# Seven half-block products for the middle half of an output projection, with the weight sums made in DRAM

## The chip, the cores and the metric

The kernel runs on one core of a Trainium2 chip. Its engines are TensorE (PE, with its weight loads shown as PEld), VectorE (DVE), ScalarE (ACT), GpSimd (POOL) and the queue engine SyncE (SP), which issues nearly all DMAs. The metric is the device time of one execution in microseconds (us), as the median of several.

## The reference

The reference is one decoder layer on 512 tokens of width 2048. It normalizes the input, projects it with `w_in`, runs two groups of eight attention heads of width 128 side by side (latent attention with a rotary key, and forgetting attention with a decay in the logits), multiplies each head's output with a SiLU gate, and projects the 16 heads together back to 2048 columns:

```python
o = jnp.concatenate([o_mla, o_fox], axis=-1) @ w_out      # (512 x 2048) @ (2048 x 2048)
return x + _rms_norm(o, g_post)
```

All of it is float32. The change touches the product with `w_out` only.

## The kernel before

**Stages.** The four pairs of forgetting heads come first (loop over `p` at L718: projections of values, queries, keys and gates, with the attention of the pair before woven in between), then the latent projections (L779), the gates of the latent heads (L841), the four pairs of latent heads (L867), and last the output projection (L988). The text counts the pairs from 0; pair 0 of the forgetting heads is first.

**Products in three terms.** A float32 operand is split in a rounded part `hi` and a remainder `lo`, and `mm3` (L128) issues hi x hi, hi x lo and lo x hi, three matmuls of 512 columns on one bank of PSUM. `split_into` (L118) makes the parts: ACT casts the rounded one, DVE subtracts it for the remainder.

**Weights.** All weights come in chunks of at most 1024 columns per partition, 512 KB. `chunk(i)` (L231) loads four chunks ahead on SP's queue into tiles `raw` (3 buffers) and divides two chunks ahead into `whi` and `wlo` (3 buffers each): an ACT cast (L220) and a DVE subtraction (L221). A division can't write before PE is done with the chunk that had the buffer, and a load can't land before the division of the chunk that had its buffer.

**The projection.** Each of the four blocks of 512 output columns runs over 16 contraction tiles (one head each; the forgetting heads first) and 4 token tiles. A chunk of `w_out` holds two contraction tiles, so a block has 8 chunks and 16 x 4 x 3 = 192 matmuls. The attention of the last latent pair is woven into block 0 by `pump` (L350), which takes steps from the list `todo`. After each block and token tile, `square` (L942) sums the squares on ACT and `gain` (L946) multiplies with the gain row on DVE. After block 3, `finish` (L953) scales the four pieces of a token tile, adds the residual rows `xr` and stores them.

**Memory.** 28 slots of 4 KB per partition (`slot`, L95) hold the head outputs, their split parts, the gain rows and the gained pieces. Once block 0 is done, the pools of the attention are closed and a pool `op` takes their place (L1024); tile by tile it waits for what stood there. Before, it held the residual rows only.

**Order.** Each engine works through its own list in order. Outside one stretch written out by hand (L718 on, first pair), the framework that builds the program makes these lists: it plays the program through with estimated durations, gives an idle engine the ready instruction that stands first in the program, and places the waits. So an instruction may run well ahead of its place in the text where its inputs and its tile are free.

Of the kernel before, what the change touches and what calls it, by code (L numbers as in the profile page):

```python
# [24 lines left out]
HW = 128  # L25
NH = 8
# [37 lines left out]
def tile_hybrid_layer(  # L64
# [16 lines left out]
    nc = tc.nc  # L81
    pe, act, dve, pool = nc.tensor, nc.scalar, nc.vector, nc.gpsimd
# [5 lines left out]
    inner = ctx.enter_context(ExitStack())  # L88
# [39 lines left out]
    def mm3(o, ah, al, bh, bl, first, last, **kw):  # L128
        pe.matmul(o, ah, bh, start=first, stop=False, **kw)  # L129
        pe.matmul(o, ah, bl, start=False, stop=False, **kw)  # L130
        pe.matmul(o, al, bh, start=False, stop=last, **kw)  # L131
# [54 lines left out]
    def add_chunks(w, cols, nk, per, width, first_k=0, single=0):  # L186


        first = len(chunks)
        k = 0  # L190
        while k < nk:
            n = min(1 if k < single else per, nk - k)
            chunks.append((w, cols, (first_k + k) % nk, n, width))
            k += n
        return range(first, len(chunks))

# [2 lines left out]
    def load(i, small=None):  # L199

        w, cols, k, n, width = chunks[i]
        if i < 2:
            raw = slot(f"raw{i}", shape=(P, 1024))
        else:
            raw = wp.tile([P, 1024], F32, tag="raw", name=f"raw{i}")
        v = raw[:, : n * width].rearrange("p (k c) -> p k c", k=n)
        for at, off, cnt in cols:
            (nc.sync if cnt >= P or small is None else small).dma_start(
                v[:, :, at : at + cnt],
                w[0, k * P : (k + n) * P, off : off + cnt].rearrange("(k p) c -> p k c", p=P),  # L210
            )
        raws[i] = raw
# [18 lines left out]
    def chunk(i, ahead_load=4, ahead=2):  # L231
        while state["loaded"] < min(len(chunks), i + ahead_load + 1):
            load(state["loaded"])
            state["loaded"] += 1
        prepare(i + ahead)
        return ready.pop(i)
# [34 lines left out]
            }  # L271
        )

    outc = [add_chunks(w_out, [(0, 512 * p, 512)], NK, 2, 512, NH) for p in range(4)]


    gcol = cst.tile([P, NK + 10], F32, name="gcol")
# [72 lines left out]
    def pump(n=1):  # L350
        for _ in range(n):
            if todo:
                todo.popleft()()

    def drain():
        while todo:
            todo.popleft()()

    def proj_T(rng, outs, kh, kl, rate=1):

        k = 0
        n_k = sum(chunks[i][3] for i in rng)
        for i in rng:
            hi, lo = chunk(i)
            for j in range(chunks[i][3]):
                for o, rows, pick in outs:
                    mm3(o[:rows, :], pick(hi, j), pick(lo, j), kh[k], kl[k], k == 0, k == n_k - 1)
                k += 1
                pump(rate)

    def proj_V(rng, banks, kh, kl, rate=1):

        k = 0
        n_k = sum(chunks[i][3] for i in rng)
        for i in rng:
            hi, lo = chunk(i)
            for j in range(chunks[i][3]):
                for t in range(NT):
                    o, fst = piece_of(banks, t, chunks[i][4])
                    ts = slice(t * P, (t + 1) * P)  # L380
                    mm3(
                        o, kh[k][:, ts], kl[k][:, ts], hi[:, j, :], lo[:, j, :],
                        k == 0 and fst, k == n_k - 1, skip_group_check=True,
                    )
                k += 1
                pump(rate)

    def piece_of(banks, t, width):

# [530 lines left out]


    order = [o_of[n // 2][:, n % 2, :] for n in range(2 * NH)]
    gps = [slot(f"gp{c}") for c in range(2)]
    gp = [gps[c // 2][:, c % 2, :] for c in range(4)]
    for c in range(4):
        nc.sync.dma_start(gp[c], g_post[:, c * 512 : (c + 1) * 512].to_broadcast([P, 512]))
    parts = {}

    def o_parts(n):
        if n not in parts:  # L930
            parts[n] = split(order[n], f"os{n}")
        return parts[n]

    og = [[None] * 4 for _ in range(NT)]
# [5 lines left out]
    og_of, xr_of = {}, {}  # L940

    def square(t, c, o):  # L942
        jt = wp.tile([P, S], F32, tag="sq", name=f"osq{c}{t}", bufs=1)
        act.activation(jt, o, AF.Square, accum_out=sso[:, t, c : c + 1])

    def gain(t, c, o):  # L946

        if t % 2 == 0:
            og_of[t // 2, c] = slot(f"og{c}{t}")
        og[t][c] = o if c == 3 or t == NT - 1 and c > 0 else og_of[t // 2, c][:, t % 2, :]  # L950
        dve.tensor_tensor(out=og[t][c], in0=o, in1=gp[c], op=ALU.mult)

    def finish(t, o):  # L953
        v, y, w, u, h = (cst.tile([P, 1], F32, name=f"fin{s}{t}") for s in "vywuh")
        dve.tensor_reduce(out=u, in_=sso[:, t, 0:3], op=ALU.add, axis=AX.X)
        dve.tensor_scalar(out=u, in0=u, scalar1=1.0 / D, scalar2=EPS, op0=ALU.mult, op1=ALU.add)
        square(t, 3, o)
        dve.tensor_scalar(out=v, in0=sso[:, t, 3:4], scalar1=1.0 / D, scalar2=u, op0=ALU.mult, op1=ALU.add)
        act.sqrt(w, v)
        dve.tensor_scalar(out=h, in0=v, scalar1=-0.5, scalar2=None, op0=ALU.mult)  # L960
        gain(t, 3, o)
# [18 lines left out]
    def load_xr(t):  # L980
        for c in range(4):
            if c % 2 == 0:
                xr_of[t] = op.tile([P, 2, S], F32, tag="xr", name=f"xr{t}{c}", bufs=8)
            xr[t][c] = xr_of[t][:, c % 2, :]
            nc.sync.dma_start(xr[t][c], x[piece(t, c)])

    last = 3
    for c in range(4):  # L988
        ob = [att_bank(f"o{c}{t}") if t == NT - 1 and c in (1, 2) else proj_bank(f"o{c}{t}") for t in range(NT)]
        rng = list(outc[c])  # L990
        held = rng[-last:] if c == 3 else []
        n = 0

        def products(t, hi, lo, n, j):
            oh, ol = o_parts(n)
            ts = slice(t * P, (t + 1) * P)
            mm3(ob[t], oh[:, ts], ol[:, ts], hi[:, j, :], lo[:, j, :], n == 0, n == 2 * NH - 1)

        if c == 3:
            load_xr(0)  # L1000
        for i in rng[: len(rng) - len(held)]:
            hi, lo = chunk(i)
            for j in range(2):
                if n == 2 * NH - 2 and c == 0:
                    drain()
                for t in range(NT):
                    products(t, hi, lo, n, j)
                n += 1
                pump(2)
        if held:  # L1010
            w = [chunk(i, ahead=0) for i in held]
            for t in range(1, NT):
                load_xr(t)
        for t in range(NT):
            for m in range(2 * len(held)):
                products(t, *w[m // 2], n + m, m % 2)
            if held:
                finish(t, ob[t])
            else:
                square(t, c, ob[t])  # L1020
                gain(t, c, ob[t])
        if c == 0:
            inner.close()
            op = ctx.enter_context(tc.tile_pool(name="op", bufs=1, reuse_waits="tile"))  # L1024


# [33 lines left out]
```

## Time and profile before

| | us |
|---|---|
| median of 3 executions | 943.79 (943.67 to 945.33) |
| the profiled execution | 945.21 |
| its span | 943.1 |
| PE busy | 932.8 |
| DVE busy | 500.8 |
| ACT busy | 343.4 |
| POOL busy | 22.6 |
| output projection, first to last matmul | 748.0 to 934.3 |

The span runs from the first to the last instruction of the profiled execution. Matmuls are pipelined, so that one is shown with 389 ns although they follow each other faster; the pace is read from the distance of events that wait for PE. "Idle before, releaser" in a row is the time in which the engine stood still before these instructions and what ended it.

### The profile page before, as it was taken

How to read it: one execution, taken by the hardware profiler on the slowest of the kernel's cores; microseconds unless marked ns; L12 is line 12 of the kernel's file. 1: busy time of each engine (PE TensorE's matmuls, PEld its weight loads, DVE VectorE, ACT ScalarE, POOL GpSimd, SP SyncE). 2: the span in 40 equal slices, each digit the busy share in tenths (PEclk: the TensorE clock that was granted, in tenths of full speed). 3: DMA queues.
4: the chain of work that ended last, by engine and by line, in shares of the span. 5: the costliest groups of instructions: out<-in, count | busy, mean ns of one | idle time of the engine just before them, and what ended most of it. 6: DMA issues, size and time to landing. Idle time of an engine off the chain costs nothing.

```text
span 943.1 us, 11667 instructions
## 1 busy us (share of the span) xinstructions
PE 932.8 (99%) x4568; PEld 792.0 (84%) x4568; DVE 500.8 (53%) x898; ACT 343.4 (36%) x639; POOL 22.6 (2%) x28
## 2 busy tenths in 40 slices
PE   9999999999999999999999999999999999999996
PEld 8888888998889888888888888888888888888885
DVE  3477743467742743742322348668887973332325
ACT  5772432233312522321211253535445642232224
POOL 1000000000000000000000040000000000000003
PEclk9999999999999999999999999999999999999999
DMA  9343323332233332333333333322222324622214
GB/s 296 87 114 110 94 86 90 112 90 83 74 105 108 90 90 80 100 90 111 90 92 110 89 90 84 93 60 73 62 73 73 112 68 148 203 96 90 94 63 179
DMA packets 88474, 95.48 MB, mean 101 GB/s; under 512 B 12482, under 2 KB 72412, under 8 KB 88420
## 3 DMA queue, kind: packets, MB, share of 16 engines
q1 hardware_dynamic: 87684, 94.35, 33.4%
q8 instruction: 36, 0.59, 0.3%
q10 hardware_dynamic: 736, 0.40, 0.2%
q14 instruction: 18, 0.15, 0.1%
HBM read 90.52 MB, written 4.21 MB: 100 GB/s over the span
## 4 chain that ended last, share of the span: by engine, by line
PE 97%; DVE 2%; ACT 0%; issue 0%; DVEq 0%; ACTq 0%
PE o L129 6%; PE o L131 6%; PE o L130 6%; PE fv L418 4%; PE l L130 4%; PE l L129 4%; PE l L131 4%; PE fg L129 3%; PE fq L129 3%; PE fq L131 3%; PE fq L130 3%; PE fg L130 3%; PE gm L129 3%; PE fg L131 3%; PE fk L131 3%; PE fk L129 3%
## 5 line engine op out<-in xcount | busy, mean ns | idle before, releaser
L221 DVE TENSOR_TENSOR wlo<-raw,whi 128x1024 fp32r<-128x1024 f32 (+3 forms) x157 | 186.4, 1189 | 299.8 <-ACT whi L220 295.2
L220 ACT CAST whi<-raw 128x1024 fp32r<-128x1024 f32 (+3 forms) x157 | 158.9, 1013 | 410.5 <-PE o L131 94.9
L129 PE MATMUL o<-whi,os 128*128 128x512 f32 x256 | 100.6, 393 | 0.0
L130 PE MATMUL o<-wlo,os 128*128 128x512 f32 x256 | 99.8, 390 | 0.0
L131 PE MATMUL o<-whi,os 128*128 128x512 f32 x256 | 99.3, 390 | 0.0
L129 PE MATMUL l<-h,whi 128*128 128x512 f32 x160 | 62.2, 389 | 0.0
L130 PE MATMUL l<-h,whi 128*128 128x512 f32 x160 | 62.2, 389 | 0.0
L131 PE MATMUL l<-h,wlo 128*128 128x512 f32 x160 | 62.2, 389 | 0.0
L131 PEld LDWEIGHTS o<-whi,os 128*128 128x128 f32 x256 | 48.0, 188 | 10.3 <-DVE os L121 0.2
L130 PEld LDWEIGHTS o<-wlo,os 128*128 128x128 f32 x256 | 48.1, 188 | 9.8
L129 PEld LDWEIGHTS o<-whi,os 128*128 128x128 f32 x256 | 48.1, 188 | 9.7
L129 PE MATMUL fq<-h,whi 128*128 128x512 f32 x128 | 52.7, 412 | 0.0
L129 PE MATMUL fg<-h,whi 128*128 128x512 f32 x128 | 50.4, 394 | 0.0
L131 PE MATMUL fq<-h,wlo 128*128 128x512 f32 x128 | 50.2, 392 | 0.0
L130 PE MATMUL fq<-h,whi 128*128 128x512 f32 x128 | 50.2, 392 | 0.0
L129 PE MATMUL fk<-h,whi 128*128 128x512 f32 x128 | 50.1, 391 | 0.0
L130 PE MATMUL fg<-h,whi 128*128 128x512 f32 x128 | 50.0, 390 | 0.0
L131 PE MATMUL fg<-h,wlo 128*128 128x512 f32 x128 | 49.9, 390 | 0.0
L129 PE MATMUL gm<-h,whi 128*128 128x512 f32 x128 | 49.9, 390 | 0.0
L131 PE MATMUL gm<-h,wlo 128*128 128x512 f32 x128 | 49.9, 389 | 0.0
L131 PE MATMUL fk<-h,wlo 128*128 128x512 f32 x128 | 49.8, 389 | 0.0
L130 PE MATMUL gm<-h,whi 128*128 128x512 f32 x128 | 49.8, 389 | 0.0
(319 smaller groups left out, 1841.3 us busy)
## 6 DMA issues: line engine op xcount, KB each, us to landing
raw<-in_w_in_dram SPq DMA_DIRECT2D x88, 512.0 KB, 3.6
raw<-in_w_out_dram SPq DMA_DIRECT2D x32, 512.0 KB, 3.6
raw<-in_w_ukv_dram SPq DMA_DIRECT2D x8, 512.0 KB, 4.0
xr<-in_x_dram SPq DMA_DIRECT2D x16, 256.0 KB, 5.2
out_dram<-og SPq DMA_DIRECT2D x15, 256.0 KB, 2.6
xa<-in_x_dram SPq DMA_DIRECT2D x7, 512.0 KB, 7.2
raw<-in_w_in_dram SPq DMA_DIRECT2D x8, 384.0 KB, 3.2
raw<-in_w_uq_dram SPq DMA_DIRECT2D x24, 128.0 KB, 2.2
```

What stands on the lines that cost most here:

```text
L129: pe.matmul(o, ah, bh, start=first, stop=False, **kw)
L130: pe.matmul(o, ah, bl, start=False, stop=False, **kw)
L131: pe.matmul(o, al, bh, start=False, stop=last, **kw)
L220: act.copy(hi[:, :m], raw[:, :m])
L221: dve.tensor_tensor(out=lo[:, :m], in0=raw[:, :m], in1=hi[:, :m].bitcast(F32), op=ALU.subtract)
L418: pe.matmul(banks[t][:, :n], a[k][:, tss[t]], b[:, j, :], start=k == 0 and m == 0, stop=k == NK - 1 and m == 2,)
```

## The change

The columns 512 to 1535 of the product, so far two blocks of 512, are computed together as a 2 x 2 block product by the scheme of Winograd and Strassen. Tokens 0 to 255 and 256 to 511 are the row halves of the heads' output A, head pairs `K1` = 0, 1, 4, 5 and `K2` = 2, 3, 6, 7 its column halves, and `w_out` has the same halves of rows and the two blocks as columns. Seven products of 256 tokens, 1024 contraction rows and 512 columns take the place of eight. In the order in which they run: p1 = A11 B11, p4 = A22 t4, p2 = A12 B21, q6 = s6 t6, g5 = s5 t5, g7 = s7 t7, g3 = s3 B22, where

- t7 = B12 + B22, t5 = B11 + B12, t6 = B11 + t7, t4 = B21 + t6 (weights),
- s5 = A21 - A22, s6 = A11 - s5, s3 = A12 - s6, s7 = A21 - A11 (heads),
- C11 = p1 + p2, C21 = p4 + p1 - (q6 + g7), C12 = q6 - p1 + (g5 + g3), C22 = g5 - p1 + (q6 + g7).

A product that stands second in a bracket goes on adding in the same PSUM bank; the rest is combined by DVE. Blocks 0 and 3 stay as they are.

The weight sums are made in DRAM, four pieces of 512 KB for each, 16 in all. `add_blocks` issues for one piece a 64-byte DMA from a weight tile in SBUF into the destination (a marker, which ties the step to its place in the program), a copy of the first operand on SP, both DRAM to DRAM apart from the marker, and a DMA from POOL that adds the second operand. `behind` issues one such step at every eighth contraction tile of the projections, once the first pair of heads is done: `proj_T` and `proj_V` call it. The head sums are made by `sum_steps`: per pair of head pairs 4 subtractions and 4 splits, the two groups of forgetting heads during block 0 (written to slots), the two of latent heads during p1 and p4 (raw sums in PSUM banks, parts in the pool `op`). The pool `op` now has 13 tiles and also holds the gain rows, loaded after block 0 in the program, the gained pieces of block 0 and four groups of parts. The number of `w_out` chunks goes from 32 to 44.

```diff
+    K1, K2 = (0, 1, 4, 5), (2, 3, 6, 7)
+    def add_blocks(name, j, first, second, mark):
+        to = W[name][j].rearrange("p (k c) -> p k c", k=2)
+        nc.sync.dma_start(W[name][j][0:1, 0:16], mark)
+        nc.sync.dma_start(to, first)
+        pool.dma_start(to, second, accum_op=ALU.add)
...
+        for step in (
+            ("t7", j, b12, b22), ("t5", j, b11, b12), ("t6", j, b11, chain["t7"]), ("t4", j, b21, chain["t6"]),
+        ):
+            bg.append(lambda mark, step=step: add_blocks(*step, mark))
...
+    outc = {0: add_plain(range(NH), 0)}
+    outp = {
+        "p1": add_plain(K1, 1), "p4": add_sums("t4"), "p2": add_plain(K2, 1), "q6": add_sums("t6"),
+        "g5": add_sums("t5"), "g7": add_sums("t7"), "g3": add_plain(K2, 2),
+    }
+    outc[3] = add_plain(range(NH), 3)
...
+    def behind(k, w):
+        if done and bg and k % 8 == 0:
+            bg.popleft()(w[0:1, 0, 0:16].bitcast(F32))
...
-    gps = [slot(f"gp{c}") for c in range(2)]
...
+        def make(n, x, y):
+            raw[n] = raw_of(f"{n}{j}").rearrange("p (h c) -> p h c", h=2)
+            dve.tensor_tensor(out=raw[n], in0=x, in1=raw[y] if isinstance(y, str) else y, op=ALU.subtract)
+        def part(n):
+            both = place(f"s{n}{j}").rearrange("p x (h c) -> p x h c", h=2)
+            split_into(both[:, 0], both[:, 1], raw[n])
+            sums[n][j] = both
+        return [
+            lambda: make("g5", a21, a22), lambda: make("q6", a11, "g5"), lambda: part("g5"), lambda: part("q6"),
+            lambda: make("g3", a12, "q6"), lambda: part("g3"), lambda: make("g7", a21, a11), lambda: part("g7"),
+        ]
...
              pump(2)
+            if n >= 4:
+                for _ in range(2):
+                    if steps:
+                        steps.popleft()()
...
+    inner.close()
+    op = ctx.enter_context(tc.tile_pool(name="op", bufs=13, reuse_waits="tile"))
+    gps = [late(f"gp{c}") for c in range(2)]
...
+    def product(name, of, o, first, last):
+        kk = 0
+        for i in outp[name]:
+            hi, lo = chunk(i)
+            for j in range(2):
+                for t, (ah, al) in enumerate(of(kk)):
+                    mm3(o[t], ah, al, hi[:, j, :], lo[:, j, :], first and kk == 0, last and kk == 7,
+                        skip_group_check=True)
+                kk += 1
+                pump()
...
+    for j in range(2, 4):
+        todo.extend(sum_steps(j, bank_temp, lambda n: late(n, F32R)))
+    product("p1", block((0, 1), K1), A, True, True)
+    p1 = slot("p1")
+    for t in range(2):
+        act.copy(p1[:, t, :], A[t])
+    B = [proj_bank(f"ob{t}") for t in range(2)]
+    product("p4", block((2, 3), K2), B, True, True)
+    f = og_of[1, 1] = slot("c21")
+    for t in range(2):
+        dve.tensor_tensor(out=f[:, t, :], in0=B[t], in1=p1[:, t, :], op=ALU.add)
+    product("p2", block((0, 1), K2), A, False, True)
...
+    product("g7", summed("g7"), C, False, True)
+    homes = {c: att_bank(f"oh{c}") for c in (1, 2)}
+    for t in range(2):
+        dve.tensor_tensor(out=e[:, t, :], in0=C[t], in1=e[:, t, :], op=ALU.add)
+        dve.tensor_tensor(out=f[:, t, :], in0=f[:, t, :], in1=C[t], op=ALU.subtract)
+    for t in range(2):
+        for c, o in ((1, f), (2, e)):
+            square(2 + t, c, o[:, t, :])
+            gain(2 + t, c, o[:, t, :], homes[c] if t else None)
+    product("g3", summed("g3"), G, False, True)
```

More of the change, by code (lines that the diff above doesn't have):

```diff
@@ L938, in piece, with late @@
         return (0, slice(t * P, (t + 1) * P), slice(c * 512, (c + 1) * 512))
-    og_of, xr_of = {}, {}
+    def late(name, dt=F32, shape=(P, 2, S)):
+        return op.tile(list(shape), dt, tag="e", name=name)
+    og_of, xr_of, gp = {}, {}, {}
     def square(t, c, o):
@@ new lines, in tile_hybrid_layer, with block, of @@
+    while steps:
+        steps.popleft()()
+    inner.close()
+    op = ctx.enter_context(tc.tile_pool(name="op", bufs=13, reuse_waits="tile"))
+    gps = [late(f"gp{c}") for c in range(2)]
+    for c in range(4):
+        gp[c] = gps[c // 2][:, c % 2, :]
+        nc.sync.dma_start(gp[c], g_post[:, c * 512 : (c + 1) * 512].to_broadcast([P, 512]))
+    for t in range(NT):
+        square(t, 0, ob[t])
+        gain(t, 0, ob[t], place=late)
+    def block(tokens, half):
+        def of(kk):
+            n = 2 * half[kk // 2] + kk % 2
+            return [tuple(a[:, t * P : (t + 1) * P] for a in o_parts(n)) for t in tokens]
+        return of
@@ L1008, in tile_hybrid_layer @@
[L1008 to L1024, printed above, removed]
+                for t, (ah, al) in enumerate(of(kk)):
+                    mm3(
+                        o[t], ah, al, hi[:, j, :], lo[:, j, :], first and kk == 0, last and kk == 7,
+                        skip_group_check=True,
+                    )
@@ L1028 @@
+    n = 0
+    load_xr(0)
+    for i in rng[:-last]:
+        hi, lo = chunk(i)
+        for j in range(2):
+            for t in range(NT):
+                products(ob[t], t, hi, lo, n, j)
+            n += 1
+    w = [chunk(i, ahead=0) for i in held]
+    for t in range(1, NT):
+        load_xr(t)
+    for t in range(NT):
+        for m in range(2 * last):
+            products(ob[t], t, *w[m // 2], n + m, m % 2)
+        finish(t, ob[t])
 _INS = [
```

125 lines of the change are left out of this document (98 added, 27 removed).

## The prediction

> **What bounds the kernel now.** I read four views in this order: the page, the waits of PE, the busy time of each engine by stage, and the timelines of ACT and DVE in the output projection. The page comes first (engine: busy time and share), then its chain:
>
> ```profile
> span 943.1 us, 11667 instructions
> PE 932.8 (99%) x4568; PEld 792.0 (84%) x4568; DVE 500.8 (53%) x898; ACT 343.4 (36%) x639; POOL 22.6 (2%) x28
> PE 97%; DVE 2%; ACT 0%; issue 0%; DVEq 0%; ACTq 0%
> ```
>
> PE is busy for 99% of the span and is 97% of the chain. The waits of PE (who waited for whom, total, times, longest) are two, both in the first microseconds, and PEld has one of 0.2 us:
>
> ```profile
> PE warm L148 <- DVE warm L143: 1.1, 1, 1.1
> PE xt L306 <- DVE h L124: 0.7, 1, 0.7
> PEld o L131 <- DVE os L121: 0.2, 1, 0.2
> ```
>
> So every matmul taken away shortens the run, as long as the other engines still feed PE. Busy time by stage (length; then PE, PEld, DVE, ACT, POOL; granted clock, DMA share, GB/s) shows what room they have:
>
> ```profile
> 125.00:334.00 209.00, 209.00 (x1100) 183.08 (x1099) 111.70 (x211) 67.16 (x117) 0.00 (x0) 1.00 0.33 94
> 759.00:770.00 11.00, 11.00 (x59) 9.46 (x58) 10.39 (x28) 5.07 (x13) 0.00 (x0) 1.00 0.31 98
> 770.00:803.00 33.00, 33.00 (x158) 27.51 (x157) 10.96 (x15) 9.31 (x16) 0.00 (x0) 1.00 0.41 133
> 803.00:889.00 86.00, 86.00 (x381) 71.22 (x380) 24.96 (x24) 21.30 (x30) 0.00 (x0) 1.00 0.36 121
> 889.00:934.00 45.00, 45.00 (x200) 37.29 (x199) 18.84 (x42) 16.54 (x30) 5.37 (x5) 1.00 0.26 90
> ```
>
> The first row is forgetting pairs 1 and 2, where the new DMAs go; the next two are the first column block of the projection with the last attention heads; the fourth is the two middle blocks that change. There DVE works 25 us of 86, ACT 21, and the DMA engines are at 36%.
>
> **The gain.** The ACT timeline of the middle blocks (start, duration, line, what; in brackets the idle time before) shows the pace:
>
> ```profile
> 809.58 1.05 ACT L220 CAST whi<-raw 128x1024 fp32r<-128x1024 f32 x1 [3.68 <-PE o L131]
> 815.02 1.05 ACT L220 CAST whi<-raw 128x1024 fp32r<-128x1024 f32 x1 [4.38 <-PE o L131]
> 820.46 1.05 ACT L220 CAST whi<-raw 128x1024 fp32r<-128x1024 f32 x1 [4.38 <-PE o L131]
> ```
>
> Each cast waits until PE has finished a chunk, and they come every 5.44 us. A chunk is 2 contraction tiles x 4 token tiles x 3 terms = 24 matmuls, so a matmul costs 5.44 / 24 = 0.2267 us. Before, the middle takes 8 half-block products of 8 x 2 x 3 = 48 matmuls, 384 in all (87.0 us). After it takes 7 x 48 = 336. **Removed: 48 x 0.2267 = 10.9 us of PE.** The new matmuls have the same 512-column shape, so I give them the same price.
>
> **What feeding costs now.** A chunk serves only two token tiles in the half products, so PE eats one every 2.72 us, and there are 28 chunks in place of 16. Durations of the other engines by group, and then one division and one square from the timelines:
>
> ```profile
> L221 DVE TENSOR_TENSOR wlo<-raw,whi 128x1024 fp32r<-128x1024 f32 x16 | 19.6, 1225 | 58.1 <-ACT whi L220 58.1
> L220 ACT CAST whi<-raw 128x1024 fp32r<-128x1024 f32 x17 | 17.9, 1053 | 60.0 <-PE o L131 60.0
> L951 DVE TENSOR_TENSOR og<-o,gp 128x512 f32<-128x512 f32 x10 | 6.9, 692 | 5.6 <-ACT osq L944 5.4
> L121 DVE TENSOR_TENSOR os<-gm,os 128x512 fp32r<-128x512 f32 x8 | 5.5, 683 | 0.0
> L120 ACT CAST os<-gm 128x512 fp32r<-128x512 f32 x8 | 4.7, 644 | 0.2 <-DVE gm L505 0.2
> 810.66 1.23 DVE L221 TENSOR_TENSOR wlo<-raw,whi 128x1024 fp32r<-128x1024 f32 x1 [3.51 <-ACT whi L220]
> ...
> 802.10 0.60 ACT L944 ACTIVATE osq<-o 128x512 f32<-128x512 f32 x1 [2.30 <-PE o L131]
> 802.59 0.19 ACT L944 ACTIVATION_READ_ACCUMULATOR osq<-o 128x1 f32 x1
> ```
>
> A division takes 1.08 + 1.23 = 2.31 us from cast to remainder. It starts when PE frees one of three buffers and must end two chunks later, 5.44 us: a margin of 3.1 us. Stage totals fit: DVE 28 x 1.225 + 12 combining additions and 12 gains x 0.692 + 16 sum steps of heads 4 to 7 x 0.683 = 62 us of 76; ACT 28 x 1.053, 12 squares at 0.79, 8 casts x 0.644 and 2 copies = 45 us. What can hurt is bunching.
>
> *First two products.* DVE: 8 divisions 9.8, the 16 sum steps 10.9, 4 gains 2.8, 2 additions 1.4 = 24.9 us in 21.8. The excess, 3.1 us, equals the margin, and the planner can put part of the sums earlier, since DVE idles 22 us of 770 to 803. I take 0.5 us; bounds 0 and 3.1. The copy of the first product needs a free slot, which the sums of the third pair group give back; it waits in ACT's queue with the next casts behind it, inside the same bounds.
>
> *After the sixth product*, 4 additions and 4 gains (5.5 us of DVE) start 0.7 us before that product's end and stand before a division: 5.5 - 0.7 + 1.2 = 6.0 us against 5.44. I take 0.9 us; bounds 0 and 2.
>
> *First column block.* Sixteen more sum steps of the forgetting heads: 10.9 us on DVE, 8 x 0.64 = 5.2 on ACT, into the 22 and 24 us that are idle from 770 to 803. Cost 0. Placed in 759 to 770, where DVE is busy 10.39 of 11 us, the eight steps of one group would delay what they precede by 5.4 us; with the margin of 3.1 that is at most 2.3 us.
>
> The gain rows move to memory that the closed attention pools give back:
>
> ```profile
> 793.23 0.69 DVE L505 TENSOR_TENSOR gm<-pvm,gm 128x512 f32<-128x512 f32 x1 [5.04 <-PE pvm L499]
> 802.82 2.87 DVE L951 TENSOR_TENSOR og<-o,gp 128x512 f32<-128x512 f32 x4 [1.76 <-ACT osq L944]
> gp<-in_g_post_dram SPq DMA_DIRECT2D x4, 256.0 KB, 5.1
> ```
>
> The attention ends at 793.2 us, they land 5.1 us after issue, and the first gain runs at 802.8, which leaves 4.5 us. A late one would hold DVE's queue, with the divisions behind it.
>
> *Loads.* Three raw buffers; a cycle is issue 0.37 + landing + division 2.31. Landing times, first in the middle blocks, then as groups (16 residual rows; 5 weight loads from 785 to 812 us, with the rate of that stretch; 7 inputs at the start):
>
> ```profile
> DMA to landing us min/median/max: 3.6/3.7/5.0
> xr<-in_x_dram SPq DMA_DIRECT2D x16, 256.0 KB, 5.2
> raw<-in_w_out_dram SPq DMA_DIRECT2D x5, 512.0 KB, 4.5
> DMA packets 3358, 6.24 MB, mean 231 GB/s; under 512 B 314, under 2 KB 314, under 8 KB 3358
> xa<-in_x_dram SPq DMA_DIRECT2D x7, 512.0 KB, 7.2
> L208 SPq DMA_DIRECT2D raw<-in_w_out_dram x13: 368/368/379, 787.9 to 855.4; - x13
> ```
>
> At 3.7 us the pace is (0.37 + 3.7 + 2.31) / 3 = 2.13 us, at 5.0 it is 2.56, both under 2.72. The rate needed is 512 KB / 2.72 us = 193 GB/s. The residual rows, 4 MB, now wait for tiles that products 4 to 7 free: groups of 1 MB between loads, each delaying one load about 3.2 us (at 324 GB/s: 133 / 0.41 in the stage table), which the margin absorbs. Cost 0; upper bound below, with 7.2 us.
>
> *Forgetting heads.* The queries' first weight loads of pair 1 and of pair 3 (count, durations, first and last start), the smallest weight loads by landing time, and POOL's first work after the start:
>
> ```profile
> L129 PEld LDWEIGHTS fq<-h,whi x17: 187/188/190, 125.6 to 139.9; 128*128 128x128 f32 x17
> L129 PEld LDWEIGHTS fq<-h,whi x14: 187/188/190, 333.5 to 344.7; 128*128 128x128 f32 x14
> raw<-in_w_uq_dram SPq DMA_DIRECT2D x24, 64.0 KB, 2.1
> L800 POOL TENSOR_TENSOR ls<-ls,lqq 128x512 f32<-128x512 f32 x5 | 6.6, 1318 | 540.9 <-ACT lqq L798 540.6
> ```
>
> Sixteen steps, at every eighth contraction tile of pairs 1 and 2, so one in 209 / 16 = 13 us. Each puts on SP a 64-byte marker from a weight tile and a 512 KB copy that waits for the marker (about 2.1 us, the landing time of the smallest weight loads), and on POOL an adding DMA that waits for the copy. Behind them on SP stand the weight loads; a raw buffer has 3 x 5.44 - 2.31 = 14.0 us to be filled, less 0.37 + 3.7, so 9.9 us to spare. Behind them on POOL stands nothing until 540.9 us. The sums are first read near 810 us. No row shows an adding DMA. Lower bound: 3.6 us like a plain 512 KB load; I know no upper one, only the point at which it matters (rival 3). I take 0, nearest to the plain load. [...]
>
> **Sum.** -10.9 + 0.5 + 0.9 = -9.5 us. The profiled execution took 945.21 us (943.1 span and 2.1 around it), 1.4 above the median of 943.79. On the median: **934.3 us**.
>
> **Rivals.**
> 1. *Bunching bites deeper.* Upper bounds together: 3.1 + 2 + 2.3 = 7.4, plus a late residual group or so; 937 to 942 us. For it: DVE at 95% or more through two products, and order fixed ahead. Against: margins of 3.1 us per chunk, and DVE idle for 22 us just before.
> 2. *Loads set the pace of the middle* (slower). Place: the three raw buffers. If a 512 KB load lands in 7.2 us, as at the kernel's start, the pace is (0.37 + 7.2 + 2.31) / 3 = 3.29 us and 28 chunks lose 28 x 0.57 = 16 us: 943.8 - 10.9 + 16 = **949 us**. It decides from a landing time of 6.65 us, where the loss is 0.39 a chunk. For it: 193 GB/s plus 4.2 MB of residual rows over four products (43.5 us, 96 GB/s) is 289. Against: 4.5 us at 231 GB/s in 785 to 812.
> 3. *Adding DMAs starve the forgetting heads.* If copy and addition hold the engines so long that loads wait over 9.9 us in each of 16 steps, PE stops there. An addition of 12 us, beside 1.6 for the copy, would cost 16 x (12 + 1.6 - 9.9) = 59 us at most, less what interleaves; 945 to 990. Against: 33% DMA share, and 13 us between steps.
> 4. *The change doesn't do what it says:* PE's matmuls fall by 48 but the middle ends when it did, a new wait taking 9 to 12.8 us: 942 to 945.7.
>
> **How the numbers follow.** Forecast, 932.5 to 937: 0.60. Rival 1, 937 to 942: 0.21. Rival 4: 0.06. Rival 2: 0.08. Rival 3: 0.05. Low end: the whole 10.9 us and nothing lost is 932.9, less the spread of runs, 932.0. The high end takes in rival 1, 942.0; that leaves out 0.19. Within 0.2% is 941.9 to 945.7, which is what a measurement of this kernel can't tell from no change: 0.06. Faster 0.60 + 0.21 = 0.81; slower 0.08 + 0.05 = 0.13.
>
> **What would show it.** Right: 48 matmuls fewer; PE still busy at 99%; casts in the middle 2.72 us apart; no PE wait for whi or wlo over 2 us; raw loads landing under 5 us; the forgetting pairs still ending near 334 us. Wrong: PE waiting on wlo in every chunk with DVE idle (loads, rival 2) or DVE busy (rival 1); the stage 125 to 334 longer (rival 3); clock below 1.00 where PE pauses.

## The result and the profile after

| | before | after |
|---|---|---|
| median, us | 944.44 (943.67 to 945.33, 4 executions) | 932.08 (931.93 to 932.79, 4 executions) |
| the profiled execution, us | 945.21 | 932.0 |
| its span, us | 943.1 | 930.2 |
| matmuls | 4568 | 4520 |

The ratio is 0.987, with a 95% interval from 0.9853 to 0.9887. The kernel is faster by 12.4 us in these executions and by 11.1 us in a second set (the run of the changed kernel again, below). The forecast was 934.3, the range 932.0 to 942.0: the time lies inside, 0.08 us from the low end. One execution of the kernel before, among those beside the experiments, took 1163 us at a granted clock of 0.75 and is left out of all that follows.

The page of the changed kernel, first the lines on busy time (engine: busy time, share, instructions) and on the chain of work that ended last, then the waits of PE, which are all there are:

```profile
PE 920.3 (99%) x4520; PEld 781.6 (84%) x4520; DVE 540.9 (58%) x954; ACT 365.5 (39%) x669; POOL 38.7 (4%) x44
PE 97%; DVE 1%; DMA 1%; ACT 0%; issue 0%; SPq 0%; DVEq 0%; ACTq 0%
```

```profile
PE warm L148 <- DVE warm L143: 1.1, 1, 1.1
PE xt L361 <- DMA xa<-in_x_dram: 0.5, 1, 0.5
```

PE has 48 matmuls fewer, DVE 40 us more work, and PE waits nowhere after its first microseconds: no wait for `whi` or `wlo` anywhere in 930 us. By stage (length; busy time of PE, PEld, DVE, ACT, POOL; granted clock, DMA share, GB/s): the forgetting pairs with the 16 steps, block 0, and the seven products.

```profile
125.00:334.00 209.00, 209.00 (x1102) 183.05 (x1101) 112.14 (x212) 67.90 (x119) 16.13 (x16) 1.00 0.68 171
770.00:803.00 33.00, 33.00 (x159) 27.51 (x158) 19.17 (x28) 14.90 (x30) 0.00 (x0) 1.00 0.32 112
802.00:878.20 76.20, 76.20 (x338) 63.02 (x337) 54.19 (x66) 38.81 (x54) 0.00 (x0) 1.00 0.70 235
```

The last row's bounds come from the first matmul of the first product and the last of the last (first and last start in each row):

```profile
L129 PE MATMUL oa<-whi,os x32: 389/389/390, 802.1 to 834.0; 128*128 128x512 f32 x32
...
L131 PE MATMUL od<-whi,sg x32: 389/389/393, 846.0 to 878.0; 128*128 128x512 f32 x32
```

From 802.1 to the end of the matmul that starts at 878.0 it is about 76.2 us, and 7 x 48 x 0.2267 is 76.2. The middle lost nothing to its feeding. The ACT timeline shows the pace of the casts, 2.72 us, released by PE and not by a load; only the last two of the middle wait for loads, the second of them for 3.71 us:

```profile
851.23 1.05 ACT L226 CAST whi<-raw 128x1024 fp32r<-128x1024 f32 x1 [1.67 <-PE od L131]
853.95 1.05 ACT L226 CAST whi<-raw 128x1024 fp32r<-128x1024 f32 x1 [1.67 <-PE od L131]
...
877.94 1.05 ACT L226 CAST whi<-raw 128x1024 fp32r<-128x1024 f32 x1 [3.71 <-DMA raw<-in_w_out_dram]
```

Between the weight loads SP issues the residual rows, mostly one or two at a time, but the last four (1 MB) in a row:

```profile
867.64 4.53 SPq L1081 DMA_DIRECT2D xr<-in_x_dram  x4
```

The next weight load is issued at 873.14, when a late division (at 871.86, below) has freed its buffer, and the cast at 877.94 is the one that waits for it. PE reaches that chunk only at 883.7 us, so it does not wait.

**The two stretches that the ledger had charged.** The DVE timeline at the first two products (802.1 to about 824) and after the sixth product:

```profile
804.21 1.21 DVE L227 TENSOR_TENSOR wlo<-raw,whi 128x1024 fp32r<-128x1024 f32 x1
805.35 0.69 DVE L1004 TENSOR_TENSOR q<-gm,g 128x512 f32<-128x512 f32 x1
806.08 1.23 DVE L227 TENSOR_TENSOR wlo<-raw,whi 128x1024 fp32r<-128x1024 f32 x1
807.22 0.68 DVE L121 TENSOR_TENSOR sg<-g,sg 128x512 fp32r<-128x512 f32 x1
...
820.86 1.28 DVE L121 TENSOR_TENSOR sg<-g,sg 128x512 fp32r<-128x512 f32 x2
...
867.06 0.69 DVE L1181 TENSOR_TENSOR c<-oc,c 128x512 f32<-128x512 f32 x1
...
871.86 3.63 DVE L227 TENSOR_TENSOR wlo<-raw,whi 128x1024 fp32r<-128x1024 f32 x3
```

In the first stretch the divisions (L227) stand between the sum steps (L1004, L121), after every one to three of them, and although DVE is busy for 21.1 of the 21.8 us from 802.1 to 823.9, PE has no wait. All 16 sum steps ran there, from 803.0 to 822.1. Adjacent instructions start closer together than their durations: 1.14 us after a division of 1.21 (804.21 to 805.35), 0.60 after a sum step of 0.68 (807.22 to the next at 807.82). In the second stretch, eight additions and gains do stand ahead of a division, as forecast: from 867.06 to 871.86 is 4.8 us (5.5 was counted), and the three divisions behind them are done by 875.5. The PE timeline shows what happens at that place:

```profile
872.79 0.61 PE L129 MATMUL od<-whi,sg 128*128 128x512 f32 x2
873.24 0.40 PE L130 MATMUL od<-wlo,sg 128*128 128x512 f32 x1
```

PE begins the chunk at 872.79 with two hi x hi matmuls (L129) in a row, for two token tiles, and only then, at 873.24, the first one that needs the remainder; the pace of 0.23 us is kept. The chunks before it begin with one. The remainder was done at about 873.1 (871.86 and a division of 1.2), 0.3 us after the chunk began.

**Where the 12.9 us of span came from.** The group of the first query projection starts at 55.1 us before and at 53.2 after; the last `o` matmul with this line starts at 933.8 and 921.1:

```profile
L129 PE MATMUL fq<-h,whi x128: 387/395/481, 55.1 to 360.7; 128*128 128x512 f32 x128
L129 PE MATMUL o<-whi,os x256: 387/389/501, 748.0 to 933.8; 128*128 128x512 f32 x128
```

```profile
L129 PE MATMUL fq<-h,whi x128: 387/395/481, 53.2 to 358.8; 128*128 128x512 f32 x128
L129 PE MATMUL o<-whi,os x128: 387/389/483, 744.7 to 921.1; 128*128 128x512 f32 x128
```

Between these two matmuls lie 878.7 us before and 867.9 after, a difference of 10.8 us, which is the 48 matmuls. The forgetting heads' queries take 305.6 us in both: the adding DMAs cost them nothing. Of the other 2.1 us, 1.9 are gone before 53 us, at the start, which the change does not touch. The PE timelines of the start (start, duration) show how, before and after:

```profile
4.13 1.11 PE L306 MATMUL xt<-ident,xa 128*128 128x128 f32 x4
...
6.81 1.09 PE L306 MATMUL xt<-ident,xa 128*128 128x128 f32 x4 [0.71 <-DVE h L124]
7.55 3.27 PE L418 MATMUL fv<-whi,h 128*128 128x456 f32 x8
10.66 0.98 PE L418 MATMUL fv<-wlo,h 128*128 128x456 f32 x4
```

```profile
6.62 0.63 PE L361 MATMUL xt<-ident,xa 128*128 128x128 f32 x4 [0.52 <-DMA xa<-in_x_dram]
7.01 1.92 PE L480 MATMUL fv<-whi,h 128*128 128x456 f32 x8
8.77 0.99 PE L480 MATMUL fv<-wlo,h 128*128 128x456 f32 x4
```

The first eight projection matmuls ran at about half the pace in the profiled execution before (from 7.55 to 10.66 us, 0.39 each) against after (from 7.01 to 8.77, 0.22 each); before, the pace rises at about 10.7 us (4 in 0.98). Whether this belongs to the change, the first experiments ask.

### The profile page after: what moved, and what is told of

Its sections match the earlier page's. It is cut to its first block, busy times and chain, and to the rows that moved or that the text cites. A ratio compares the mean times of both kernels' runs of the same rounds, so it can differ in the third digit from the quotient of the medians.

```text
span 930.2 us, 11809 instructions
## 1 busy us (share of the span) xinstructions
PE 920.3 (99%) x4520; PEld 781.6 (84%) x4520; DVE 540.9 (58%) x954; ACT 365.5 (39%) x669; POOL 38.7 (4%) x44
## 4 chain that ended last, share of the span: by engine, by line
PE 97%; DVE 1%; DMA 1%; ACT 0%; issue 0%; SPq 0%; DVEq 0%; ACTq 0%
PE fv L480 4%; PE l L131 4%; PE l L130 4%; PE l L129 4%; PE fg L129 3%; PE fq L129 3%; PE fq L131 3%; PE fq L130 3%; PE o L131 3%; PE o L129 3%; PE fg L130 3%; PE fg L131 3%; PE o L130 3%; PE gm L129 3%; PE fk L129 3%; PE gm L130 3%
## 5 line engine op out<-in xcount | busy, mean ns | idle before, releaser
L227 DVE TENSOR_TENSOR wlo<-raw,whi 128x1024 fp32r<-128x1024 f32 (+3 forms) x169 | 201.0, 1191 | 249.6 <-ACT whi L226 244.6
L226 ACT CAST whi<-raw 128x1024 fp32r<-128x1024 f32 (+3 forms) x169 | 171.5, 1016 | 381.4 <-PE l L130 83.3
L129 PE MATMUL l<-h,whi 128*128 128x512 f32 x160 | 62.3, 389 | 0.0
L129 PE MATMUL fq<-h,whi 128*128 128x512 f32 x128 | 52.7, 412 | 0.0
L129 PE MATMUL o<-whi,os 128*128 128x512 f32 x128 | 50.9, 397 | 0.0
L129 PE MATMUL fg<-h,whi 128*128 128x512 f32 x128 | 50.4, 394 | 0.0
L129 PE MATMUL fk<-h,whi 128*128 128x512 f32 x128 | 50.1, 391 | 0.0
L130 PE MATMUL o<-wlo,os 128*128 128x512 f32 x128 | 50.0, 390 | 0.0
L129 PE MATMUL gm<-h,whi 128*128 128x512 f32 x128 | 49.9, 390 | 0.0
L131 PE MATMUL o<-whi,os 128*128 128x512 f32 x128 | 49.9, 390 | 0.0
L130 PE MATMUL fk<-h,whi 128*128 128x512 f32 x128 | 49.8, 389 | 0.0
L131 PE MATMUL fv<-whi,h 128*128 128x256 f32 (+1 forms) x128 | 39.5, 309 | 0.0
L130 PE MATMUL fv<-wlo,h 128*128 128x256 f32 (+1 forms) x128 | 39.5, 309 | 0.0
```

What stands on the lines that cost most here:

```text
L226: act.copy(hi[:, :m], raw[:, :m])
L227: dve.tensor_tensor(out=lo[:, :m], in0=raw[:, :m], in1=hi[:, :m].bitcast(F32), op=ALU.subtract)
```

## The experiments

Three theories stood at the outset. For the 10.9 us: that they are the matmuls and nothing else, with every other cost hidden. For the rest of the 12.4: that the start has two levels by chance, or that the change moves the start. Against the hidden costs: the rivals of the prediction, each with the cover taken away that had made it nothing. Ratios are to the kernel before on the same chip.

### The start: the kernel before again, with more filler, and the changed kernel again

The kernel before, unchanged:

> The kernel before, unchanged, to read its start once more. In the profile of the change everything from 53 us on is 10.9 us shorter in all, as 48 matmuls of 0.2267 us ask for; another 1.9 us lie in the first 55 us, where the change touched nothing: the first eight value matmuls take 3.27 us in the profile before and 1.92 us after. Theory A, chance of the execution (the array's pace in its first microseconds): the times of this kernel lie on two levels some 1.5 us apart, and a profile shows either 3.3 or 1.9 us for those eight matmuls, with a span near 943.1 or near 941.5. Theory B, the change quickened the start: this profile shows 3.3 us again and a span near 943.1, and all its times lie near 945.2.

The kernel before with more filler matmuls in the first pause of PE:

```diff
-        idle(2)
+        idle(4)
         x_turn(1)
```

> The kernel before with four filler matmuls instead of two ahead of the second input tile, so that PE has work from 1.1 us on until that tile has landed (before, it stands still for 0.7 to 1.0 us there). In the slower start the first eight value matmuls take 3.27 us instead of 1.92. Theory A, that is the array at half pace until it has been busy without a pause for some microseconds, and the pause decides it: no times near 945.2 any more, all within 943.2 to 944.3. Theory B, the pause has nothing to do with it: two levels as before, four of ten near 945.2, or all some 0.3 us later for the filler.

The changed kernel, unchanged:

> The change, unchanged, for more of its times and a second profile. The kernel before has times on two levels, about 943.5 (14 of 25 beside the first experiments) and 945.2 us (10 of 25); the four times of the change lie within 931.9 to 932.8. Theory A, both kernels start by the same chance and the gain on a level is the 10.9 us of the matmuls: two levels here too, near 932.3 and 934, four of ten or so on the upper one. Theory B, the change keeps to the lower level: all times below 933.

Measured:

| | median, us | ratio | executions |
|---|---|---|---|
| before again | 944.43 | 1.0 (0.999 to 1.001) | 10: five from 943.22 to 943.9, one at 944.96, four from 945.3 to 945.65 |
| before with filler | 943.63 | 0.9994 (0.9985 to 1.0003) | 11, 943.0 to 944.49 |
| changed again | 932.63 | 0.9881 (0.9868 to 0.9895) | 932.47, 932.54, 932.73, 933.58 |

The executions of the kernel before that ran beside these fall in the same two groups, 943.1 to 944.2 and 945.0 to 945.8, with 10 of 24 and 6 of 21 in the upper one. The profiled execution of the unchanged kernel, at 943.59 us, and that with filler (the PE timelines of the two):

```profile
6.96 0.63 PE L306 MATMUL xt<-ident,xa 128*128 128x128 f32 x4 [0.86 <-DMA xa<-in_x_dram]
7.35 1.90 PE L418 MATMUL fv<-whi,h 128*128 128x456 f32 x8
9.09 0.99 PE L418 MATMUL fv<-wlo,h 128*128 128x456 f32 x4
```

```profile
4.13 0.66 PE L306 MATMUL xt<-ident,xa 128*128 128x128 f32 x4
4.63 1.06 PE L148 MATMUL warm<-warm 128*128 128x128 f32 x8
```

So the kernel before has both levels without any change; its execution at 943.59 starts at full pace, the one at 945.21 at half pace. The span of that faster one is 941.5 us, and 941.5 - 930.2 = 11.3 us: 10.9 for the matmuls, 0.34 for the second input tile, whose transposes came 0.34 us earlier (6.62 against 6.96), and 0.1 left over. The second profile of the changed kernel gives the same: its span is 930.9 us and its transposes come at 7.28, and 941.5 - 930.9 + (7.28 - 6.96) is 10.9. With filler no execution is near 945.2, where 6 of the 21 of the kernel before that ran beside it are. Eleven misses at that rate would come by chance in 2 to 3% of cases ((15/21)^11), so the times speak for the theory that it is decided by how busy PE is in its first microseconds. The profile does not show it: the first transposes run at the higher pace already (four in 0.66 us from 4.13 us on, against 1.11 us at the same time in the profile of before), ahead of the added filler, which starts behind them at 4.63; and PE's pause before the second transposes is still there, 1.4 us against 0.71.

The changed kernel showed no upper level in 8 executions, 931.93 to 933.58. It was expected to show one now and then; with 21 of 55 executions of the kernel before in the upper group, 8 misses would come by chance in about 2% of cases ((34/55)^8). One of the eight, at 933.58, lies above the 933 of theory B and below the 934 of theory A, so neither was met in full. Why there is no upper level stays open, and it shows that a set without the upper group is no proof for the filler either. Among ten executions of the variant with two load buffers (below), one at 945.4 lies 1.2 us above the other nine, as the upper group would. What stands is the comparison level with level: 943.6 for the lower group of before (its median), less 10.9, is 932.7, and the second set of the changed kernel has 932.63.

Half pace lasted to about 10.7 us in the one profiled execution of the upper group; in the nine others the second transposes, which start between 6.62 and 7.45 us, already run at the higher pace (four in 0.63 us against 1.09). From the start of these transposes to the first matmuls with `wlo`, the slow start takes 3.85 us (6.81 to 10.66) and the quick one of the same kernel 2.13 (6.96 to 9.09), so 1.72 us less. The groups lie about 1.7 us apart (near 943.6 and 945.3). What ends the half pace is not shown here, and of the upper group only one execution was profiled.

### Eight halves instead of seven products

The changed kernel's tiling, chunks and order with the eight ordinary half products: 32 chunks in the middle, no head sums, no weight sums, no adding DMAs.

```diff
-    outp = {
-        "p1": add_plain(K1, 1), "p4": add_sums("t4"), "p2": add_plain(K2, 1), "q6": add_sums("t6"),
-        "g5": add_sums("t5"), "g7": add_sums("t7"), "g3": add_plain(K2, 2),
-    }
+    outp = {}
+    for c in (1, 2):
+        for h in range(2):
+            for m, pairs in enumerate((K1, K2)):
+                outp[c, h, m] = add_plain(pairs, c)
...
+    for (c, h), kind in kinds.items():
+        o = [kind[t](f"oq{c}{h}{t}") for t in range(2)]
+        tokens = (2 * h, 2 * h + 1)
+        product((c, h, 0), block(tokens, K1), o, True, False)
+        product((c, h, 1), block(tokens, K2), o, False, True)
```

> The two middle blocks as eight ordinary half products of 256 tokens and half of the contraction, in the same order of loads and with the same tiles, without weight sums, head sums and combining additions. So it has the change's pace of chunks (12 matmuls each, 32 chunks in the middle where the change has 28) and the matmuls of before. Theory A, feeding at 2.72 us a chunk is free: the time of before, 943.8 within 1.5 us, PE without waits. Theory B, part of the gain is lost in feeding: each of 32 chunks late by some 0.05 to 0.5 us, 945.5 to 960.

Measured: 944.0 us (943.47 to 945.48), ratio 0.9999 (0.999 to 1.0008). Its middle by stage, and the loads that were issued in it:

```profile
802.00:889.00 87.00, 87.00 (x385) 72.05 (x384) 45.36 (x45) 38.85 (x49) 0.00 (x0) 1.00 0.70 236
```

```profile
DMA to landing us min/median/max: 3.5/4.3/6.0
```

Twice as many chunks, each used for half as long, cost nothing: 87.0 us for 384 matmuls, as before the change, at the DMA share and rate that the seven products have (0.70 and 235). So the whole gain is the eighth product, and not something in the new order. Loads took 4.3 us at the median where the prediction had 3.7 from the quieter middle, and the pace that the three buffers allow at that landing, (0.37 + 4.3 + 2.31) / 3 = 2.33 us, is still under 2.72.

### Only the adding DMAs

The kernel before with the 16 steps in DRAM issued as in the change, and their sums read by nobody.

```diff
+    def behind(k, w):
+        if done and bg and k % 8 == 0:
+            bg.popleft()(w[0:1, 0, 0:16].bitcast(F32))
...
                 pump(rate)
+                behind(k, hi)
```

> The kernel before plus the sixteen steps of marker, copy and adding DMA in pairs 1 and 2 of the forgetting heads; nobody reads the sums. Theory A, they are hidden: the time of before within 0.2%, while the DMA share of 125 to 334 us rises from 0.33 to near 0.68. Theory B, they cost something that the profile of the change hides behind its quicker start: 1 to 3 us more than before. Theory C, they quicken something: 1 to 2 us less than before.

Measured: 943.95 us (943.05 to 945.57), ratio 0.9999 (0.999 to 1.0009). The stage of the two pairs, by the same columns:

```profile
125.00:334.00 209.00, 209.00 (x1102) 183.05 (x1101) 112.14 (x212) 67.94 (x120) 16.05 (x16) 1.00 0.68 171
```

The DMA share is 0.68 instead of 0.33 and PE has no gap. What one step costs the DMA engines follows: (0.68 - 0.33) x 209 / 16 = 4.6 us of all sixteen. The page of the changed kernel gives what no row of before showed, the time from issue to landing of the adding DMAs (source `w_out`, then a sum as source); in it POOL is busy 16.13 us for the 16 issues, 1.0 us each:

```profile
t<-in_w_out_dram POOLq DMA_DIRECT2D x8, 512.0 KB, 6.9
t<-t POOLq DMA_DIRECT2D x8, 512.0 KB, 5.7
```

### A step at every contraction tile

The changed kernel with a step at every contraction tile in place of every eighth; the weights' sums and their use are the same.

```diff
-        if done and bg and k % 8 == 0:
+        if done and bg:
```

> The change with one step of marker, copy and adding DMA at every contraction tile of the forgetting heads, in place of every eighth, so all sixteen fall into some 28 us at the start of pair 1. In the change the sixteen steps raise the DMA share of 209 us from 0.33 to 0.68, which is 4.6 us of all engines a step, 73 us in all. Theory A, adding DMAs and loads share the engines packet by packet and a load has 9.9 us to spare: within 2 us of the change, 931 to 934. Theory B, loads queue behind the copies and behind SP's waits for them, and PE stops: 945 to 975, with the loss between 125 and 220 us.

Measured: 950.21 us (949.54 to 950.83), ratio 1.0065 (1.0052 to 1.0079), 18 us over the change. By stage, then PE's longest wait, the ACT timeline around it, and PE's matmuls just after it:

```profile
125.00:150.00 25.00, 25.00 (x124) 20.49 (x123) 8.08 (x12) 5.82 (x11) 4.04 (x4) 1.00 0.98 232
150.00:175.00 25.00, 9.73 (x36) 7.60 (x35) 4.74 (x7) 2.72 (x5) 4.03 (x4) 0.66 1.04 246
175.00:200.00 25.00, 25.00 (x144) 22.12 (x143) 8.44 (x9) 6.19 (x7) 4.88 (x5) 1.00 1.07 259
```

```profile
PE pvf L129 <- ACT phf L120: 14.5, 1, 14.5
```

```profile
163.49 1.04 ACT L226 CAST whi<-raw 128x1024 fp32r<-128x1024 f32 x1 [21.16 <-DMA t<-in_w_out_dram]
164.44 0.37 ACT L120 CAST phf<-ptf 128x256 fp32r<-128x256 f32 x1
```

```profile
166.77 0.63 PE L129 MATMUL fq<-h,whi 128*128 128x512 f32 x1
167.19 0.63 PE L130 MATMUL fq<-h,whi 128*128 128x512 f32 x1
167.62 0.63 PE L131 MATMUL fq<-h,wlo 128*128 128x512 f32 x1
```

The DMA engines are full from 125 to 200 us (share 0.98 to 1.07). ACT waits 21.16 us with a weight cast at the head of its queue until a DMA of a step is through; the attention's cast stands behind it, needing none of this, and PE waits for that cast for 14.5 us. The granted clock of the stretch is 0.66, and just after the pause matmuls of 512 columns start 0.42 to 0.43 us apart (166.77, 167.19, 167.62) in place of 0.2267. The adding DMAs with `w_out` as source landed after 12.3 us here, those with a sum as source after 8.1:

```profile
t<-in_w_out_dram POOLq DMA_DIRECT2D x8, 512.0 KB, 12.3
t<-t POOLq DMA_DIRECT2D x8, 512.0 KB, 8.1
```

So the steps can starve the forgetting heads, as rival 3 said, and the spacing of 13 us keeps that away; but it came by another path than the rival's, since the longest wait is that of a cast for a DMA of a step and not for a weight load. Which of a step's three DMAs held the cast isn't shown for certain. Only the marker reads a weight tile, which makes it likely; two other casts of this stretch did wait for a marker (7.6 us the longer one), and SP issued the next copy, which waits for its marker, 0.13 us before this cast began. No run isolates it. The adding DMAs from `w_out` took 12.3 us at a DMA share of 0.98 to 1.07, in place of 6.9 at 0.68.

### The latent head sums twice

The changed kernel with every DVE instruction of the latent groups' 16 sum steps issued a second time (the same result written again): 10.9 us more on DVE, over the first two products if the ledger's window is right.

```diff
-            dve.tensor_tensor(out=raw[n], in0=x, in1=raw[y] if isinstance(y, str) else y, op=ALU.subtract)
+            for _ in range(2 if j > 1 else 1):
+                dve.tensor_tensor(out=raw[n], in0=x, in1=raw[y] if isinstance(y, str) else y, op=ALU.subtract)
...
+            if j > 1:
+                dve.tensor_tensor(out=both[:, 1], in0=raw[n], in1=both[:, 0].bitcast(F32), op=ALU.subtract)
```

> The change with each DVE instruction of the sixteen sum steps of the latent heads issued twice (the second writes the same values again), so 16 x 0.68 = 10.9 us more of DVE work within the first two of the seven products. By the ledger of the prediction DVE then has 24.9 + 10.9 = 35.8 us to do in 21.8. Theory A, DVE's room of 3.1 us a chunk is the margin that saved the change, and it is used up: 932.1 + 10.9 - (0 to 3) = 940 to 943, with PE waiting for wlo there. Theory B, the sums run ahead in the idle time before or give way to the divisions, since they are first needed by the fourth product: 932 to 935.

Measured: 933.9 us (933.46 to 934.06), ratio 0.989 (0.9875 to 0.9904): 1.3 us over the second set of the changed kernel and 1.8 over the first, for 10.9 us of work. Its PE waits beside the one of every kernel here (1.1 us at the start), and the last sum step on DVE:

```profile
PE xt L361 <- DMA xa<-in_x_dram: 1.7, 1, 1.7
...
PE oc L129 <- ACT whi L226: 0.8, 1, 0.8
```

```profile
838.70 0.68 DVE L1011 TENSOR_TENSOR sg<-g,sg 128x512 fp32r<-128x512 f32 x1
```

The sums run on to 839 us, over the third product and into the fourth, with divisions between them; PE shows one wait, 0.8 us for a chunk of the fourth product. The first product to read such sums is that one (q6), so the end of the second was no deadline. Against the first profile of the changed kernel, 0.7 us belong to the start, where the second input tile came late (1.7 us against 0.5). The first matmul of the middle begins at 802.8 and the last at 880.1, 77.3 us apart; in that profile of the changed kernel they begin at 802.1 and 878.0, 75.9 us apart. So the middle did lose 1.4 us to the doubled sums.

### Two load buffers

The changed kernel with two `raw` tiles for weight loads in place of three.

```diff
-            raw = wp.tile([P, 1024], F32, tag="raw", name=f"raw{i}")
+            raw = wp.tile([P, 1024], F32, tag="raw", name=f"raw{i}", bufs=2)
```

> The change with two load buffers for weights in place of three, to see how far the loads are from setting the pace in the middle. A load of 512 KB lands in 4.3 us (median) at this rate, as the run with eight half products shows, so with two buffers a chunk takes at least (0.37 + 4.3 + 2.31) / 2 = 3.49 us against 2.72 that PE needs; outside the middle chunks last 4.1 us or more and two buffers do. Theory A, the cycle of a load buffer is as in the prediction: 28 x 0.77 = 21.6 less some 3 us of lead, 932 + 18 to 22 = 950 to 954. Theory B, it is looser than that (transfers of two loads overlap, or the planner orders them better): under 940.

Measured: 943.7 us (943.34 to 945.4), ratio 0.9998 (0.9989 to 1.0007), 11.1 to 11.6 us over the change. Waits of ACT, the largest group of PE's waits, and the end of the last product:

```profile
ACT whi L226 <- DMA raw<-t: 23.9, 13, 3.9
ACT whi L226 <- DMA raw<-in_w_out_dram: 19.6, 9, 3.5
```

```profile
PE od L130 <- DVE wlo L227: 2.7, 6, 0.8
```

```profile
L131 PE MATMUL od<-whi,sg x32: 388/390/398, 850.4 to 889.6; 128*128 128x512 f32 x32
```

The middle now lasts from 802.3 to about 889.8, 87.5 us, 3.12 us a chunk, and nearly all casts that wait do so for loads and not for PE: the place and the signature of rival 2. PE's waits for `whi` and `wlo` in it sum to 6.0 of the 11.3 us that were lost; a matmul is shown 0.16 us longer than the pace (0.39 against 0.23), so a late one is seen in part only. I had expected 950 to 954 under this reading, from a landing of 4.3 us; by the cycle of two buffers, 3.12 x 2 = 0.37 + landing + 2.31, the landing would be 3.6 us. That is solved for and not read, and it takes in the start of the middle, where PE lost nothing until 823 us. The eight casts between 853 and 878 us start 3.3 to 5.2 us after the issue of their load, 4.2 on average, which makes the landing some 3.8 us and the chunk (4.2 + 2.31) / 2 = 3.25 us; over the 20 chunks behind 823 us that is 20 x 0.53 = 10.6 us. So my 4.3 was too long. The 4.3 was measured with three buffers at 236 GB/s, and with two the middle moved 203 GB/s; no run isolates why the landing is shorter. One buffer is thus worth the whole gain of the eighth product.

## Why the prediction was right, and where it was wrong

**The gain, 10.9 us: right.** The middle is 76.2 us for 336 matmuls, eight halves with the same tiling take 87.0, and from 55 us on the two traces differ by 10.8. The step that gave the new matmuls the price of the old ones holds.

**First two products, +0.5: too much, measured 0.** The ledger found 24.9 us of DVE work in 21.8, and so an excess of 3.1. The work did run there: all 16 sum steps, and none of them earlier, where the ledger had hoped to see a part. Two of the ledger's steps fail. First, it added durations, and adjacent instructions on DVE start closer than that: at the distances shown above, the same list is 8 x 1.14 + 22 x 0.60 = 22.3 us, an excess of 0.5, which the margin of 3.1 covers. The 0.5 us that it charged was a choice between bounds, and the likeness of the two figures is chance. Second, it closed the window at the end of the second product, though the first product to read these sums is the fourth, and the planner put divisions between them as they came due. The doubled sums show that: DVE got 10.9 us more by the durations, the steps ran on to 839 us, and the middle lost 1.4 us.

**After the sixth product, +0.9: too much, measured 0 in PE's waits.** The order was as forecast, eight instructions ahead of a division. They took 4.8 us instead of 5.5, since adjacent ones on DVE start 0.60 us apart and not 0.69, but they began 0.3 us before the product's end (867.35) and not 0.7, behind a division. So the sum is 4.8 - 0.3 + 1.2 = 5.7 us, still over 5.44. What hid it is a cover that the ledger doesn't have: of a chunk PE does hi x hi first, and at this chunk two of them, so that the remainder is needed 0.45 us after the chunk begins and not at its first matmul.

**Block 0, loads, forgetting heads, gain rows, each 0: right.** In block 0 DVE went from 10.96 to 19.17 us of 33, with no PE wait. Of its sixteen sum steps eleven ran before 770 us, from 741 on, and not in the idle time behind it; that was the placement for which the ledger had a bound of 2.3 us, and it cost nothing on PE. Of the residual rows one group of 1 MB did come in a row, behind the sixth product, and a cast waited 3.71 us for the load behind it; the margin absorbed that, as forecast. The sign "raw loads landing under 5 us" can't be read, since the profile of the changed kernel gives no landing times for its weight loads; that load reached its cast 4.8 us after its issue. The adding DMAs landed in 5.7 to 6.9 us, about twice the lower bound of 3.6, and hid in the spacing of 13 us. Two readings in the prediction are loose without an effect on the sum: PEld's single wait of 0.2 us holds for the output projection alone (over the whole kernel PEld has about twenty short waits, up to 1.1 us), and 540.9 us is the length of POOL's pause, which ends at 543.6.

**The base.** The sum was put on the median of three executions, 943.79, which is one of the quicker start, while the profile shown was of the slower one (the prediction left the 1.4 us between them unexplained). With the median of the lower group, 943.6 - 10.9 = 932.7. The two charges above make up the 1.4 us by which the forecast stood over the 932.9 with nothing lost. The measured 932.08 lies below that too, and the low end of the range held, by 0.08 us, only because the spread of runs had been added to it: that part is luck.

**Rivals.** Rival 1 (bunching) is refuted for this kernel: its condition came true (DVE busy 21.1 of 21.8 us, the order fixed ahead) and its loss did not, and with 10.9 us of further DVE work it cost 1.4 us. Rival 4 (a new wait in place of the old) is refuted by the waits of PE. Rival 2 (loads) is real with two buffers. Starved forgetting heads, rival 3, are real with dense steps, by way of a held cast. Both are kept away by a choice of the change, not by a lack of the mechanism.

## What to carry to other kernels

In this kernel, with TensorE busy 99% of the time, seven block products in place of eight gave their full eighth, because what each chunk needs from the other engines fitted the halved time per chunk; three load buffers and additions in DRAM spread 13 us apart were what made that true, and either cover taken away cost 11 to 18 us. When you charge work to a window, price adjacent instructions by the distance of their starts and not by their durations (on DVE here 0.60 us and not 0.68 at 128x512), and close the window where a consumer first reads the result, not where the program text has the work. Before you subtract a profile from a median, look whether the first microseconds of that execution are those of the typical one.

## What the hardware showed that I had not expected

- The kernel before has two levels about 1.7 us apart, 21 of 55 executions in the upper. In the one profiled execution of the upper group the first matmuls ran at half pace up to about 10.7 us, while the granted clock was shown as 1.00 in the same microseconds. With twice the filler ahead of the second transposes none of 11 executions was in the upper group (943.63 us at the median); whether the filler is the cause stays open.
- The run with a pause of 14.5 us on PE lost 18 us in all. Just behind the pause, from 166.77 to 167.62 us, matmuls of 512 columns started 0.42 to 0.43 us apart instead of 0.2267, in a stretch with a granted clock of 0.66.
- An adding DMA from DRAM to DRAM of 512 KB lands in 5.7 to 6.9 us beside weight loads at a DMA share of 0.68, and in 12.3 us for those from `w_out` when the engines are full. Copy and addition together take 4.6 us of all sixteen engines.
- A background step that shares one tile with a compute engine can hold that engine's whole queue, 21.16 us in the dense run, by the marker or another part of the step.
- Adjacent DVE instructions start closer together than their shown durations: 0.60 us apart at 128x512 (shown with 0.68), 1.14 at 128x1024 (shown with 1.21 to 1.23).
